# Moving 128x128 transposes of a hybrid decoder layer from TensorE to VectorE and SBUF-to-SBUF transfers

## The chip, the core and the metric

The kernel runs on one core of a Trainium2 chip. The metric is the device time of one execution in microseconds (us); the time of a kernel is the median of its runs. The core has a matrix engine (TensorE, PE in the profile), a vector engine (VectorE, DVE), a scalar engine (ScalarE, ACT), GpSimd (POOL) and SyncE (SP), which issues nearly all transfers (DMAs) here. Each engine runs its own list of instructions in order; semaphores tie the lists together.

## The reference: what is computed

One decoder layer over 2048 tokens of width 1024, in float32. After an RMS norm the tokens are projected; 4 heads of a gated linear recurrence (HGRN2, key and value width 128) and 8 heads of sliding-window attention (width 64, 2 key/value heads, window 128, one sink logit per head) run side by side; their outputs are joined, projected and added to the input. Then follow a norm, a gated MLP of width 2816 with a causal convolution of 3 tokens, and a last norm.

```python
u = rmsnorm(h, norm_mix_w[l]);  proj = u @ w_in[l]
o_hg = hgrn2_chunkwise(q_hg, k_hg, v_hg, log_f)          # S_t = diag(f_t) S_{t-1} + k_t v_t^T, o_t = S_t^T q_t
...
# attention: each block of 128 queries reads its own and the previous 128 keys; dist = query - key
scores = jnp.where((dist >= 0) & (dist < WINDOW), scores, -jnp.inf)
p = jnp.exp(scores - m);  denom = jnp.sum(p) + jnp.exp(sink - m)
out = (p / denom) @ [V_prev; V_own]
...
h = h + jnp.concatenate([o_hg, o_att], -1) @ w_out[l]
h = h + (silu(conv(v @ w_gate[l])) * (v @ w_up[l])) @ w_down[l]
```

Because the window is as long as a block, of every pair (key k of the previous block, key k of the own block) a query sees exactly one. The kernel therefore keeps one 128x128 matrix of probabilities per block and head, in which each entry belongs either to the own or to the previous block.

## The kernel before, in words

The tokens are worked in two halves of 1024 (`hf` 0 and 1). Each half has a mixing part (both kinds of heads) and then the output projection and the MLP. Large products are made of three passes over numbers split into a high and a low part (`unit`, L218: 48 matmuls of 512 columns for one 128-wide projection; `pop` in the trace is such a unit of the output projection, `g`, `q`, `f`, `hq` those of the heads).

The mixing part is cut into stages. A table `ORDER` lists them: `f`, `q`, `l`, `s`, `p` for each recurrence head (gate, query, the seven levels of the within-chunk decay, the state update, the output), `qa`, `sc`, `pv`, `pw` for each of four pairs of attention heads (query projection, scores and softmax, output of the first and of the second 512 tokens), and `g`, `v`, `w`, `m` for gates, values, weight loads and splits. The table sets priorities; a scheduler of the framework then interleaves the instructions of different stages on each engine by an estimated time line, so that the order on an engine is known only from the built program.

What the change touches:

- **Probabilities.** In `attend`, stage `sc` writes the scores into `sc` (ring `sc` of two buffers), takes the row maxima (L411), eight exponentials (L421) and normalises (L426). Stages `pv` and `pw` each turn the 128x128 matrices of one group of 512 tokens on TensorE (L435, eight transposes into `ppt`), multiply the result on VectorE by two masks (L438: `po` for the own block, `pp` for the previous one) and multiply with the values (L446, `poT`: V of the previous block with `pp`, V of the own block with `po`). `po`, `pp` and the split queries `qh`, `ql` share a ring `pp` of four buffers.
- **Keys of the recurrence.** In `hgrn`, stage `s` turns the decayed keys `K` on TensorE (L564, eight transposes into `pkn`), copies them to `Kn` on ScalarE (L565) and forms the state updates (L571, `pu`, then `SS` on VectorE, L578). Stage `p` multiplies with the values (L590 and L592, `po`), takes the norm (L593 on ScalarE, then a chain of small VectorE instructions from L173 on, then L600) and turns the result back (L605, `pot`). `ST`, `Kn` and `on` share a ring `t4` of two buffers; `SS` has one.
- **What is carried from half 0 to half 1**: the last block's keys and values, in SBUF (`kc`, `vc`).
- **Weights.** Every projection's weights come by one 512 KB load on SP's queue into `raw` (three buffers, L198), are split into `whi` and `wlo` (two buffers each) and used by 48 matmuls.

Of the kernel before, what the change touches and what calls it, by code (L numbers as in the profile page):

```python
# [8 lines left out]
F32 = mybir.dt.float32  # L9
F32R = mybir.dt.float32r  # L10
# [7 lines left out]
P = 128  # L18
# [7 lines left out]
HG = 4  # L26
# [23 lines left out]
def hymba_layer(ctx: ExitStack, tc: tile.TileContext, a: dict, out: bass.AP, rows_out: bass.AP):  # L50
# [18 lines left out]
    def ps(kind, name):  # L69
        return spaces[kind].tile([P, 512], F32, tag=kind, name=name)  # L70
# [6 lines left out]

    nmw = cp.tile([P, 16], F32, name="nmw")[:, 0:KT]
    nc.scalar.dma_start(nmw, a["norm_mix_w"])
    ones = cp.tile([P, P], F32, name="ones")  # L80
    nc.vector.memset(ones, 1.0)
# [3 lines left out]
    nc.scalar.activation(warm, ones[:, 0:1], AF.Tanh)  # L85
# [13 lines left out]
    def constants():  # L99

        C.own = cp.tile([P, P], F32, name="own")
        C.ownT = cp.tile([P, P], F32, name="ownT")
        C.prevT = cp.tile([P, P], F32, name="prevT")
        for t, op, sgn in ((C.own, ALU.is_ge, 1), (C.ownT, ALU.is_ge, -1), (C.prevT, ALU.is_gt, 1)):
# [225 lines left out]
    def across(t, base, dims):  # L330

        v = t[:, :]
        return bass.AP(v.tensor, v.offset + base, [list(v.ap[0])] + dims)

    def rows(kv):
        return slice(kv * HD, (kv + 1) * HD)

    def att_keys(hf, kv, invb, p):

        KS = p.tile([P, 2, P + HALF], F32R, name="KS")
        V = p.tile([P, 1 + TT, P], F32, name="V")
        if hf:
            nc.vector.tensor_copy(KS[:, :, 0:P], kc)
            nc.vector.tensor_copy(V[:, 0], vc)
        kT, vT = [p.tile([P, HALF], F32, tag="f", name=n, bufs=2) for n in ("kT", "vT")]
        for jj, dst in ((ATT_J, kT), (ATT_J + 1, vT)):
            o = kv[jj - ATT_J]  # L350
            for b, bs in halves():
                nc.vector.tensor_tensor(blocks(dst[:, bs], b), blocks(o[b]), blocks(invb[:, bs]), op=ALU.mult)
                nc.scalar.activation(dst[:, bs], dst[:, bs], AF.Identity, bias=C.battn[:, jj:jj + 1])
        for kv in range(2):
            r, other = rows(kv), rows(1 - kv)
            nc.scalar.copy(KS[r, kv, P:], kT[r])
            nc.vector.tensor_tensor(KS[other, kv, P:], kT[r], KS[r, kv, P:].bitcast(F32), op=ALU.subtract)
        for b in range(NB):
            pv = ps("at", "pv")
            for i in range(4):  # L360
                t0 = (b * 4 + i) * P
                nc.tensor.transpose(pv[:, i * P:(i + 1) * P], vT[:, t0:t0 + P], ident)
            nc.scalar.copy(V[:, 1 + 4 * b:5 + 4 * b].rearrange("p a b -> p (a b)"), pv)
        if hf + 1 < NH:
            nc.vector.tensor_copy(kc, KS[:, :, HALF:HALF + P])
            nc.vector.tensor_copy(vc, V[:, TT])
        return KS, V

    def attend(hf, j, X, invb, KS, V, mix, p):

        o = unit(a["w_att"][j], X, "q")
        qT = slot(f"att{j}")
# [6 lines left out]
        for g in range(NB):  # L379
# [44 lines left out]
            nc.vector.tensor_tensor(den, den, es, op=ALU.add)  # L424
            nc.vector.reciprocal(den, den)
            nc.vector.tensor_tensor(sc, sc, den.unsqueeze(3).to_broadcast([P, 2, 4, P]), op=ALU.mult)  # L426
            scs.append(sc)
        yield
        for g, sc in enumerate(scs):
            pm = []  # L430
            for kv in range(2):
                pm.append([p.tile([P, 4, P], F32, tag="pp", name=n, bufs=4) for n in ("po", "pp")])
                pt = ps("at", "ppt")
                for i in range(4):
                    nc.tensor.transpose(pt[:, i * P:(i + 1) * P], sc[:, kv, i], ident)  # L435
                ptv = pt.rearrange("p (i q) -> p i q", i=4)
                for dst, mk in zip(pm[kv], (C.ownT, C.prevT)):
                    nc.vector.tensor_tensor(dst, ptv, mk.unsqueeze(1).to_broadcast([P, 4, P]), op=ALU.mult)  # L438
            oT = ps("at", "poT")
            for i in range(4):  # L440
                n = g * 4 + i
                noprev = hf == 0 and n == 0
                for prev in (0,) if noprev else (1, 0):
                    for kv in (1, 0):
                        r = rows(kv)
                        nc.tensor.matmul(oT[r, i * P:(i + 1) * P], V[:, n + 1 - prev, r], pm[kv][prev][:, i],  # L446
                                         start=noprev or prev == 1, stop=prev == 0)
# [12 lines left out]
    def hgrn(hf, h, X, invb, vs, WG, gates, mix, p, fu=None):  # L460
# [47 lines left out]
        for m in LEVELS:  # L508
# [49 lines left out]
        Kn = p.tile([P, TT, P], F32, tag="t4", name="Kn", bufs=2)  # L558
        for b in range(NB):
            pk = ps("hg", "pkn")  # L560
            n = min(4, kept - 4 * b)
            for i in range(n):
                c = slice((b * 4 + i) * P, (b * 4 + i + 1) * P)
                nc.tensor.transpose(pk[:, i * P:(i + 1) * P], K[:, c], ident)  # L564
            nc.scalar.copy(Kn[:, 4 * b:4 * b + n].rearrange("p a b -> p (a b)"), pk[:, 0:n * P])  # L565
# [537 lines left out]
    for hf in range(NH):  # L1103
        X, kv, invb, rs, f0 = nxt
        with ExitStack() as st:
            p = pool(f"mix{hf}", stack=st, reuse_waits="tile")
            KS, V = att_keys(hf, kv, invb, p)
# [4 lines left out]
            pairs = [attend(hf, h, X, invb, KS, V, mix, p) for h in range(HG)]  # L1112
# [89 lines left out]
```

## Time and profile before

| | |
|---|---|
| time, median of 3 runs (lowest to highest) | 2150.38 us (2150.18 to 2150.38) |
| profiled execution: span from first to last instruction | 2149.0 us |
| TensorE busy | 2130.8 us (99%) |
| VectorE, ScalarE busy | 1632.2 us (76%), 1020.2 us (47%) |
| mean granted TensorE clock | 0.999 |
| transfers: all queues | 254.41 MB, mean 118 GB/s |

The profiled execution's own time is taken as its span, 2149.0 us, which is 1.4 us under the median of the runs. A group row reads: line, engine, operation, output<-inputs, shape, count | busy us in all, mean ns of one | idle time before it. A timeline or chain row reads: start us, length us, engine, what, count. Matmuls overlap in the pipeline, so the length of one matmul's row is longer than the time until the next one starts; the starts of neighbouring rows give the pace. A matmul on plain float32 data has two records in the trace for one in the program; transposes and the split products have one.

### The profile page before, as it was taken

What the parts mean: (1) busy time and instruction counts of PE and PEld (TensorE: products, weight loads), DVE (VectorE), ACT (ScalarE), POOL (GpSimd) and SP (SyncE); (2) the same over time, 40 slices, a digit from 0 to 9 for tenths busy, and PEclk for the clock granted to TensorE, in tenths of its full rate; (3) what the DMA queues carried; (4) which work ended last, traced back from release to release, by engine and by line L of the source; (5) the groups of instructions that cost most, each with busy time, mean ns of one, the idle gap of its engine ahead of it and who ended that gap; (6) DMA issues with size and microseconds to landing.
All of it is one profiled execution on the core that took longest, in us unless ns stands there. A gap on an engine that the chain in (4) does not pass through costs nothing.

```text
span 2149.0 us, 29228 instructions
## 1 busy us (share of the span) xinstructions
PE 2130.8 (99%) x11271; PEld 1790.6 (83%) x11271; DVE 1632.2 (76%) x2443; ACT 1020.2 (47%) x1818; POOL 16.2 (1%) x45
## 2 busy tenths in 40 slices
PE   8999999999999999999999999999999999999998
PEld 6988988888888888888889889888888888888887
DVE  6576768788887888785775767677988888787765
ACT  5445554564444445345634446535544444443453
POOL 2000000000000000000000000000000000000000
PEclk9999999999999999999999999999999999999999
DMA  4111012413332334974641111124223323359743
GB/s 158 40 30 40 31 30 79 137 62 125 94 122 89 103 118 147 371 255 145 217 138 40 30 31 33 40 75 158 69 104 103 118 84 122 95 187 398 236 147 133
DMA packets 91147, 254.41 MB, mean 118 GB/s; under 512 B 11136, under 2 KB 13952, under 8 KB 91008
## 3 DMA queue, kind: packets, MB, share of 16 engines
q1 hardware_dynamic: 90576, 252.29, 35.3%
q8 instruction: 88, 1.44, 0.3%
q14 instruction: 51, 0.42, 0.1%
q10 hardware_dynamic: 432, 0.27, 0.0%
HBM read 195.37 MB, written 57.15 MB: 118 GB/s over the span
## 4 chain that ended last, share of the span: by engine, by line
PE 93%; DVE 5%; ACT 1%; issue 1%; DMA 0%; SPq 0%; DVEq 0%; ACTq 0%
PE X L767 7%; PE X L766 7%; PE X L765 7%; PE pop L218 6%; PE q L218 4%; PE f L218 4%; PE hq L218 4%; PE Y L767 4%; PE Y L765 4%; PE Y L766 4%; PE pdx L954 3%; PE pdx L953 3%; PE pdx L952 3%; PE g L218 3%; PE pdy L953 3%; PE pdy L954 3%
## 5 line engine op out<-in xcount | busy, mean ns | idle before, releaser
L638 ACT CAST whi<-raw 128x1024 fp32r<-128x1024 f32 x88 | 92.7, 1053 | 115.5 <-PE X L766 71.1
L765 PE MATMUL X<-T,whi 128*128 128x512 f32 x352 | 136.9, 389 | 0.0
L766 PE MATMUL X<-T,whi 128*128 128x512 f32 x352 | 136.9, 389 | 0.0
L767 PE MATMUL X<-T,wlo 128*128 128x512 f32 x352 | 136.9, 389 | 0.0
L836 DVE SCALAR_TENSOR_TENSOR y<-ga,cw,y 128x1024 f32<-128x1024 f32 x88 | 112.7, 1280 | 25.9 <-ACT y L834 25.8
L639 DVE TENSOR_TENSOR wlo<-raw,whi 128x1024 fp32r<-128x1024 f32 x88 | 107.3, 1219 | 4.4 <-ACT whi L638 4.4
L771 ACT COPY u<-X 128x512 f32<-128x512 f32 x88 | 51.6, 586 | 122.5 <-PE X L767 122.2
L199 ACT CAST whi<-raw 128x1024 fp32r<-128x1024 f32 x58 | 60.5, 1048 | 98.8 <-issue 20.6
L639 DVE TENSOR_TENSOR xld<-raw,xhd 128x1024 fp32r<-128x1024 f32 x72 | 81.1, 1132 | 17.8 <-ACT xhd L638 17.6
L638 ACT CAST xhd<-raw 128x1024 fp32r<-128x1024 f32 x72 | 69.8, 978 | 39.1 <-DMA raw<-act0T 14.0
L218 PE MATMUL pop<-XL,whi 128*128 128x512 f32 x256 | 84.2, 392 | 0.9 <-DVE XL L230 0.9
L218 PE MATMUL pop<-XH,wlo 128*128 128x512 f32 x256 | 83.3, 391 | 0.8 <-DVE wlo L200 0.8
L218 PE MATMUL pop<-XH,whi 128*128 128x512 f32 x256 | 83.1, 396 | 0.8 <-ACT XH L229 0.5
L200 DVE TENSOR_TENSOR wlo<-raw,whi 128x1024 fp32r<-128x1024 f32 x58 | 70.5, 1220 | 9.8 <-ACT whi L199 9.8
L767 PEld LDWEIGHTS X<-T,wlo 128*128 128x128 f32 x352 | 66.1, 188 | 13.7
L766 PEld LDWEIGHTS X<-T,whi 128*128 128x128 f32 x352 | 66.1, 188 | 13.7
L765 PEld LDWEIGHTS X<-T,whi 128*128 128x128 f32 x352 | 66.0, 188 | 13.7
L630 PE MATMUL pvv<-whi,XH 128*128 128x256 f32 x256 | 73.0, 286 | 0.0
L631 PE MATMUL pvv<-whi,XL 128*128 128x256 f32 x256 | 72.9, 286 | 0.0
L632 PE MATMUL pvv<-wlo,XH 128*128 128x256 f32 x256 | 71.9, 285 | 0.0
L767 PE MATMUL X<-B,wlo 128*128 128x512 f32 x176 | 68.7, 390 | 0.7 <-DVE wlo L639 0.7
L765 PE MATMUL X<-T,Sh 128*128 128x512 f32 x176 | 68.7, 390 | 0.0
(390 smaller groups left out, 6399.2 us busy)
## 6 DMA issues: line engine op xcount, KB each, us to landing
wr<-in_w_down SPq DMA_DIRECT2D x90, 512.0 KB, 5.6
raw<-in_w_gate SPq DMA_DIRECT2D x44, 512.0 KB, 3.6
raw<-in_w_up SPq DMA_DIRECT2D x44, 512.0 KB, 3.6
raw<-act0T SPq DMA_DIRECT2D x20, 512.0 KB, 5.9
raw<-act1T SPq DMA_DIRECT2D x20, 512.0 KB, 5.6
act0B<-y SPq DMA_DIRECT2D x33, 256.0 KB, 2.3
act1B<-y SPq DMA_DIRECT2D x33, 256.0 KB, 2.4
raw<-in_w_out SPq DMA_DIRECT2D x16, 512.0 KB, 3.7
```

What stands on the lines that cost most here:

```text
L218: nc.tensor.matmul(o[b], w, x[:, bs], start=f, stop=l)
L630: nc.tensor.matmul(o[:, 0:256], xh[:, t], hi[:, c], start=kt == 0, stop=False)
L631: nc.tensor.matmul(o[:, 0:256], xl[:, t], hi[:, c], start=False, stop=False)
L632: nc.tensor.matmul(o[:, 0:256], xh[:, t], lo[:, c], start=False, stop=kt == KT - 1)
L638: nc.scalar.copy(h, src)
L639: return (eng or nc.vector).tensor_tensor(l, src, h.bitcast(F32), op=ALU.subtract)
L765: nc.tensor.matmul(o, wh[:, ws], xh, start=i == 0 and not more, stop=False, skip_group_check=more)
L766: nc.tensor.matmul(o, wh[:, ws], xl, start=False, stop=False, skip_group_check=more)
L767: nc.tensor.matmul(o, wl[:, ws], xh, start=False, stop=i == 3, skip_group_check=more)
L836: nc.vector.scalar_tensor_tensor(y, g[:, w:w + HALF], C.cw[:, ft, w:w + 1], y, op0=ALU.mult, op1=ALU.add)
L953: nc.tensor.matmul(o, wh[:, i, c], al[:, i, cols], start=False, stop=False, skip_group_check=more)
L954: nc.tensor.matmul(o, wl[:, i, c], ah[:, i, cols], start=False, stop=l, skip_group_check=more)
```

## The change

For the first three of the four pairs, the probabilities are no longer turned on TensorE. Still in stage `sc`, VectorE turns every 32x32 block in place of the whole matrix (`turned`, a block transpose from `sc` to `st`, 512 columns at a time), and 16 transfers on SP's queue (`moved`) carry the 4x4 grid of blocks of `st` to their mirrored places in `pt`. `pt` takes its buffers from the ring `sc`, `st` from the ring `pp`; no ring has grown. For the first three of the four recurrence heads the keys go the same way, at the end of stage `l`: `Kd` from the ring of `SS`, then 16 transfers into `Kn`. The last pair and the last head stay on TensorE.

The mask of the previous block is gone. With P the whole turned matrix and `po` = P masked to the own block, the output is V_prev P + (V_own - V_prev) `po`; the difference `VD` is formed once per half. The last pair, which still goes through PSUM, copies P from PSUM on ScalarE (`pw`) and masks it on VectorE.

The carried keys and values go through DRAM in place of SBUF, a constant and a mask fall away, and in `ORDER` stage `q1` now stands ahead of `pv0`.

```diff
-ORDER = ("f0 q0 l0 qa0 v0 s0 f1 p0 sc0 w0 pv0 q1 l1 qa1 pw0 g0 s1 qa2 sc1 w1 m4 f2 pv1 g1 p1 m1 q2 pw1 l2 "
+ORDER = ("f0 q0 l0 qa0 v0 s0 f1 p0 sc0 w0 q1 pv0 l1 qa1 pw0 g0 s1 qa2 sc1 w1 m4 f2 pv1 g1 p1 m1 q2 pw1 l2 "
...
-    kc = cp.tile([P, 2, P], F32R, name="kcarry")
-    vc = cp.tile([P, P], F32, name="vcarry")
+    kc = dp.tile([P, 2, P], F32, name="kcarry")
+    vc = dp.tile([P, P], F32, name="vcarry")
...
+    def moved(dst, src):
+
+        for a in range(4):
+            for c in range(4):
+                nc.sync.dma_start(dst[32 * c:32 * c + 32, :, 32 * a:32 * a + 32],
+                                  src[32 * a:32 * a + 32, :, 32 * c:32 * c + 32])
+
+    def turned(dst, src):
+
+        nc.vector.transpose(dst.rearrange("p a b -> p (a b)"), src.rearrange("p a b -> p (a b)"))
...
+        VD = p.tile([P, TT, P], F32, name="VD")
+        if hf:
+            nc.vector.tensor_tensor(VD, V[:, 1:], V[:, 0:TT], op=ALU.subtract)
+        else:
+            nc.scalar.copy(VD[:, 0], V[:, 1])
+            nc.vector.tensor_tensor(VD[:, 1:], V[:, 2:], V[:, 1:TT], op=ALU.subtract)
...
             nc.vector.tensor_tensor(sc, sc, den.unsqueeze(3).to_broadcast([P, 2, 4, P]), op=ALU.mult)
+            if j < ATT_J - 1:
+                pt = p.tile([P, 8, P], F32, tag="sc", name="pt", bufs=2)
+                for kv in range(2):
+                    t = p.tile([P, 4, P], F32, tag="pp", name="st", bufs=4)
+                    turned(t, sc[:, kv])
+                    moved(pt[:, 4 * kv:4 * kv + 4], t)
+                sc = pt
...
-                pm.append([p.tile([P, 4, P], F32, tag="pp", name=n, bufs=4) for n in ("po", "pp")])
-                pt = ps("at", "ppt")
-                for i in range(4):
-                    nc.tensor.transpose(pt[:, i * P:(i + 1) * P], sc[:, kv, i], ident)
-                ptv = pt.rearrange("p (i q) -> p i q", i=4)
-                for dst, mk in zip(pm[kv], (C.ownT, C.prevT)):
-                    nc.vector.tensor_tensor(dst, ptv, mk.unsqueeze(1).to_broadcast([P, 4, P]), op=ALU.mult)
+                own.append(p.tile([P, 4, P], F32, tag="pp", name="po", bufs=4))
+                if j < ATT_J - 1:
+                    whole.append(sc[:, 4 * kv:4 * kv + 4])
+                else:
+                    pt = ps("at", "ppt")
+                    for i in range(4):
+                        nc.tensor.transpose(pt[:, i * P:(i + 1) * P], sc[:, kv, i], ident)
+                    whole.append(p.tile([P, 4, P], F32, tag="pp", name="pw", bufs=4))
+                    nc.scalar.copy(whole[kv].rearrange("p i q -> p (i q)"), pt)
+                nc.vector.tensor_tensor(own[kv], whole[kv], C.ownT.unsqueeze(1).to_broadcast([P, 4, P]), op=ALU.mult)
...
+        Kn = p.tile([P, TT, P], F32, tag="t4", name="Kn", bufs=2)
+        if h < HG - 1:
+            Kd = p.tile([P, TT, P], F32, tag="SS", name="Kd", bufs=1)
+            turned(Kd, K.rearrange("p (c t) -> p c t", t=P))
+            moved(Kn, Kd)
         yield
...
-        for b in range(NB):
+        for b in range(NB if h == HG - 1 else 0):
             pk = ps("hg", "pkn")
```

The scheduler has made another order of all stages. Three places show it. The first is TensorE near the end of the mixing part of half 0, from the transposes of head 2's output (`pot`) on; `po` ahead of it is that head's product with values and states, `pdiag` and `plev` are the levels of the last head, `psc` the scores of the last pair. Before (its `po` rows stand 54 rows further up, with `hq`, `g` and `psc` between):

```order
L218 MATMUL g0_3224<-XH_159,wlo_3220 128x512
L605 MATMUL pot_2795<-ident_85,on_2750 128x128 x4
L218 MATMUL g1_3225<-XH_159,wlo_3220 128x512
L605 MATMUL pot_2801<-ident_85,on_2750 128x128 x4
L218 MATMUL g0_3224<-XH_167,whi_3219 128x512
L218 MATMUL g1_3225<-XH_167,whi_3219 128x512
L399 MATMUL psc_3165<-KS_447,qh_3159 128x256
```

The same place in the change:

```order
L620 MATMUL po_2922<-v_2585,ST_2251 128x128
L622 MATMUL po_2922<-SS_2900,Q_2249 128x128
L635 MATMUL pot_2964<-ident_83,on_2919 128x128 x4
L635 MATMUL pot_2970<-ident_83,on_2919 128x128 x4
L512 MATMUL pdiag_3130<-hg3_3120,K_3124 64x64 x16
L543 MATMUL plev_3149<-Q_3126,G_3150 128x2x64 x4
```

The gate units `g` of heads 2 and 3 that stood around and behind `pot` have moved ahead of it, and `pot` follows its own inputs `po` at once. From the first `pot` up to the last group of turned probabilities of the last pair (`ppt`, ahead of `pw3`), the list before has 55 matmuls of `g`, 76 of `pop` and 16 of `psc`; the list of the change has none of `g`, 30 of `pop` and 32 of `psc`.

The second place is SP's queue at pair 2 of half 0 (`raw` are weight loads, `h0` a load of the input):

```order
L196 DMA raw_3689<-in_w_out 128x1024
L337 DMA Kn_2370<-Kd_2371 32x8x32 x16
L337 DMA pt_2451<-st_2452 32x4x32 x16
L337 DMA pt_2451<-st_2470 32x4x32 x16
L337 DMA pt_2548<-st_2549 32x4x32 x16
L337 DMA pt_2548<-st_2567 32x4x32 x16
L196 DMA raw_3695<-in_w_out 128x1024
L196 DMA raw_3753<-in_w_out 128x1024
L196 DMA raw_3828<-in_w_out 128x1024
L701 DMA h0_3701<-in_xT 128x1024
```

Eighty transfers of 32 partitions stand here in one run between two weight loads; before, the weight loads followed each other.

The third is ScalarE at the second projection of values in half 0 (`v_2585` and `v_2586` receive it from PSUM; `on_2103` belongs to head 1's output, `sc_1858` to pair 1's softmax):

```order
L438 ACTIVATE es_1902<-es_1902 128x8
L623 ACTIVATE on_2103,ss_2104<-po_2106 128x128
L436 ACTIVATE sc_1858,den_1905<-sc_1858,m_1899 128x128 x8
L623 ACTIVATE on_2103,ss_2104<-po_2105 128x128
L623 ACTIVATE on_2103,ss_2104<-po_2106 128x128
L664 ACTIVATE v_2586<-pvv_2599,y_358 128x128
L664 ACTIVATE v_2586<-pvv_2626,y_358 128x128
```

The value tile `v_2586` takes the buffer of head 1's values, which head 1's last `po` frees, and its eviction now stands behind eight exponentials.

More of the change, by code (lines that the diff above doesn't have):

```diff
@@ L84, in hymba_layer @@
     warm = cp.tile([P, 32], F32, name="warm")[:, 0:1]
-    nc.scalar.activation(warm, ones[:, 0:1], AF.Tanh)
+    nc.vector.memset(warm, 1.0)
+    nc.scalar.activation(warm, warm, AF.Tanh)
     nc.gpsimd.memset(ident, 1.0)
@@ L102, in constants @@
         C.ownT = cp.tile([P, P], F32, name="ownT")
-        C.prevT = cp.tile([P, P], F32, name="prevT")
-        for t, op, sgn in ((C.own, ALU.is_ge, 1), (C.ownT, ALU.is_ge, -1), (C.prevT, ALU.is_gt, 1)):
+        for t, op, sgn in ((C.own, ALU.is_ge, 1), (C.ownT, ALU.is_ge, -1)):
             nc.gpsimd.memset(t, 1.0)
@@ L429, in attend @@
         for g, sc in enumerate(scs):
-            pm = []
+            whole, own = [], []
             for kv in range(2):
-                pm.append([p.tile([P, 4, P], F32, tag="pp", name=n, bufs=4) for n in ("po", "pp")])
-                pt = ps("at", "ppt")
-                for i in range(4):
-                    nc.tensor.transpose(pt[:, i * P:(i + 1) * P], sc[:, kv, i], ident)
-                ptv = pt.rearrange("p (i q) -> p i q", i=4)
-                for dst, mk in zip(pm[kv], (C.ownT, C.prevT)):
-                    nc.vector.tensor_tensor(dst, ptv, mk.unsqueeze(1).to_broadcast([P, 4, P]), op=ALU.mult)
+                own.append(p.tile([P, 4, P], F32, tag="pp", name="po", bufs=4))
[8 more added lines that the diff above has]
+                nc.vector.tensor_tensor(own[kv], whole[kv], C.ownT.unsqueeze(1).to_broadcast([P, 4, P]), op=ALU.mult)
             oT = ps("at", "poT")
@@ L442, in attend @@
                 noprev = hf == 0 and n == 0
-                for prev in (0,) if noprev else (1, 0):
+                for w in (1,) if noprev else (0, 1):
                     for kv in (1, 0):
                         r = rows(kv)
-                        nc.tensor.matmul(oT[r, i * P:(i + 1) * P], V[:, n + 1 - prev, r], pm[kv][prev][:, i],
-                                         start=noprev or prev == 1, stop=prev == 0)
+                        vv, pr = ((V, whole), (VD, own))[w]
+                        nc.tensor.matmul(oT[r, i * P:(i + 1) * P], vv[:, n, r], pr[kv][:, i],
+                                         start=noprev or w == 0, stop=w == 1)
             gs = slice(g * 512, (g + 1) * 512)
@@ L1111, in hymba_layer @@
             heads = [hgrn(hf, h, X, invb, vs, WG, gates, mix, p, None if h else f0) for h in range(HG)]
-            pairs = [attend(hf, h, X, invb, KS, V, mix, p) for h in range(HG)]
+            pairs = [attend(hf, h, X, invb, KS, V, VD, mix, p) for h in range(HG)]
             for name in ORDER:
```

17 lines of the change are left out of this document (7 added, 10 removed).

## The prediction

> **What bounds the kernel now.** I read the head of the page first, then TensorE's waits, then the stretch in which the change reorders most.
>
> ```profile
> span 2149.0 us, 29228 instructions
> PE 2130.8 (99%) x11271; PEld 1790.6 (83%) x11271; DVE 1632.2 (76%) x2443; ACT 1020.2 (47%) x1818; POOL 16.2 (1%) x45
> PE 93%; DVE 5%; ACT 1%; issue 1%; DMA 0%; SPq 0%; DVEq 0%; ACTq 0%
> PE kv L218 <- ACT XH L232: 6.2, 2, 5.8
> PE pop L218 <- DVE XL L230: 0.9, 2, 0.6
> ```
>
> TensorE is busy for all but 18 us of the span, the chain that ended last is 93% TensorE, and of its waits (us in all, times, longest) the largest is at the start of the keys' and values' projection, the next is 0.9 us. So a matmul that is taken away shortens the run by its own pace, as long as TensorE still has something to do in its place. And a stall of TensorE has no slack to vanish in: each us that it waits is a us of the run. The sum below is therefore a ledger of TensorE alone: work removed, against idle time added.
>
> The two stretches from `pot` of head 2 to the last `ppt` of pair 3, one in each half, read so by windows:
>
> ```profile
> core 0: us, PE busy (x) PEld busy (x) DVE busy (x) ACT busy (x) POOL busy (x), PEclk, DMA share, GB/s
> 315.23:359.53 44.30, 43.19 (x311) 35.76 (x310) 39.24 (x61) 23.41 (x60) 0.00 (x0) 1.00 0.31 96
> 1379.00:1424.81 45.81, 44.72 (x322) 37.11 (x321) 40.48 (x63) 24.56 (x63) 0.00 (x0) 1.00 0.29 92
> ```
>
> Here VectorE is busy for 39.24 of 44.30 us (0.886), ten points above its mean: the levels of head 3 and the softmax of pair 3 both run on it. TensorE idles for only 1.1 us, because `g` and `pop` stand between its dependent pieces. The two engines are nearly balanced, and this is where the change takes filler away.
>
> **Part 1, transposes removed.** 96 of the 128 `ppt` transposes and 45 of the 60 `pkn` ones go (three pairs and heads of four), 141 in all.
>
> ```profile
> L435 PE MATMUL ppt<-ident,sc 128*128 128x128 f32 x128 | 18.0, 273 | 0.0
> L564 PE MATMUL pkn<-ident,K 128*128 128x128 f32 x60 | 8.2, 273 | 0.0
> 359.46 1.09 PE L435 MATMUL ppt<-ident,sc 128*128 128x128 f32 x8
> 360.31 0.48 PE L218 MATMUL pop<-XL,whi 128*128 128x512 f32 x1
> ```
>
> A row's mean of 273 ns is a length in a pipeline. The pace is read from starts: eight transposes begin at 359.46 and the next matmul at 360.31, so one costs 0.85/8 = 0.106 us. Saving: 141 x 0.106 = 15.0 us. As an upper bound I take the busy time, 18.0/128 = 0.140 each, 19.8 us; there is no lower one beneath the pace, except the cover lost, which is counted apart.
>
> The Trainium skill, "TensorE: Matmul & The Clock Gate", Part 4, gives a 128x128 transpose some 275 ns in a kernel's context and 390 ns alone (for bf16). The trace's row length of 273 ns agrees with the first, its starts do not: they come 0.106 us apart. By 390 ns the saving would be 55 us (an estimate from that page) and the time 2135 us, that of the first rival below.
>
> **Part 2, idle at `pot`.** The new order puts `pot` of head 2 directly behind `po`. Before, 11.1 us of other matmuls lay between:
>
> ```profile
> 303.80 0.39 PE L592 MATMUL po<-SS,Q 128*128 128x128 f32 x2
> 314.90 0.60 PE L605 MATMUL pot<-ident,on 128*128 128x128 f32 x4
> L593 ACT ACTIVATE on<-po 128x128 f32<-128x128 f32 x64 | 17.7, 276 | 37.5 <-PE po L592 35.8 <-ACT whi L199 0.2
> 309.10 0.17 DVE L182 TENSOR_TENSOR t<-t,ms 128x8 f32<-128x8 f32 x1
> 309.30 0.17 DVE L183 SCALAR_TENSOR_TENSOR y<-t,y 128x8 f32<-128x8 f32 x1
> 310.10 1.29 DVE L600 TENSOR_TENSOR on<-po,y 128x512 f32<-128x512 f32 x2
> ```
>
> From `po` to `pot` there is a chain: one square on ScalarE (some 0.4 with its accumulator), twelve small VectorE instructions that start 0.20 apart (2.4), then the two products with the norm (1.29): 4.1 us. Nothing stands in TensorE's list to cover it, so 4.1 us of idle time in each half. Bounds: 4.1 if VectorE is free at once, more if other rows are ahead of it there.
>
> **Part 3, the end of the mixing part.** The order rows ahead of this text count the stretch: the list of the change has 55 matmuls of `g` and 46 of `pop` fewer, and 16 of `psc` more; it also has 16 more matmuls of `poT`, 13 of `po`, 8 of `pu`, 8 of `pkn` and 4 of `ppt`. Prices:
>
> ```profile
> 371.66 8.44 PE pop L218 x37
> 253.37 0.94 PE psc L399 x8
> 282.64 1.90 PE poT L446 x32
> 280.85 1.78 PE pu L571 x16
> ```
>
> `pop` and `g`: 8.44/37 = 0.228 each, 101 of them 23.0 us. `psc` 0.117, 16 make 1.9. A `poT` or `pu` has two records: 1.90/16 = 0.119, so 1.9; 1.78/8 = 0.223, so 1.8, and with the same price for `po` 2.9. Twelve transposes 1.3. So TensorE's work in the stretch falls from 43.2 to 43.2 - 23.0 + 9.8 = 30.0 us.
>
> VectorE's list there, from the first product behind `on` to the last mask, has 72 instructions in the change: 33 of 128x512, 5 predicated copies of 128x512, 8 of 128x256, 7 of 128x1024, 8 updates of `SS`, and 11 small ones.
>
> ```profile
> 440.23 2.41 DVE T L639 x4
> 330.83 2.24 DVE XL L230 x2
> L542 DVE COPY_PREDICATED ST<-lmask,plev 128x512 f32<-128x512 uint32 x40 | 38.3, 958 | 0.2
> L408 DVE COPY_PREDICATED sc<-own,psc 128x256 f32<-128x256 uint32 x64 | 27.6, 444 | 7.4 <-ACT sc L407 5.4 <-ACT sc L405 1.7
> L578 DVE SCALAR_TENSOR_TENSOR SS<-SS,F,pu 128x128 f32<-128x128 f32 x52 | 17.9, 344 | 1.9
> ```
>
> By pace, four of 128x512 take 2.41 (0.60 each) and two of 128x1024 take 2.24 (1.12). A mean length is some 0.09 longer than the pace, since neighbours overlap (0.17 long and 0.20 apart only for the small ones). So 33 x 0.60 = 19.8; 5 x 0.87 = 4.3; 8 x 0.36 = 2.8; 7 x 1.12 = 7.9; 8 x 0.26 = 2.0; 11 x 0.20 = 2.2: 39.0 us. If VectorE is fed as well as it was (0.886), the stretch takes 39.0/0.886 = 44.0 us. TensorE has work for 30.0 of it, against 1.1 of idle before: 44.0 - 30.0 - 1.1 = 12.9 us lost in each half. Lower bound, VectorE without any gap: 39.0 - 30.0 - 1.1 = 7.9. The filler itself isn't lost: it runs earlier, where it covers pair 2's transfers.
>
> **Part 4, idle at the values.** The second values' eviction stands behind eight exponentials on ScalarE:
>
> ```profile
> 350.75 0.41 ACT L421 ACTIVATE sc<-sc,m 128x128 f32<-128x128 f32 x1
> 353.47 0.39 ACT L421 ACTIVATE sc<-sc,m 128x128 f32<-128x128 f32 x1
> ```
>
> Seven steps take 2.72, so eight 3.1. Behind that eviction wait the PSUM buffers of `pvv` and with them TensorE. Bounds 0 (the projection comes late enough anyway) to 3.1 plus two squares, 3.5; I take 3.0, since the first `pvv` needs no eviction but all behind it do.
>
> **Part 5, edits at nothing.** *Transfers.* 480 are new, 384 of 16 KB and 96 of 32 KB, and no row before shows one of 32 partitions from SBUF to SBUF. The nearest rows:
>
> ```profile
> 2135.60 3.65 SPq L1086 DMA_DIRECT2D out<-h  x8
> out<-h SPq DMA_DIRECT2D x24, 256.0 KB, 2.4
> out<-h SPq DMA_DIRECT2D x12, 64.0 KB, 1.7
> 12.68 0.33 SPq L130 DMA_DIRECT2D sinkb<-in_sinks  x1
> 13.95 0.33 SPq L132 DMA_DIRECT2D nfw<-in_norm_ffn_w  x1
> SPq L198 <- DVE wlo L200: 470.5, 38, 37.4
> ```
>
> Eight issues of 64 KB or more take 3.65 with the last one's 0.33: a pace of 0.47, landing 1.7 us later. Below lies the issue alone, 0.33; above, the 1.27 between the starts of two small loads when the queue was crowded. I take 0.47, the row nearest in size. A group of 32 then holds SP for 15 us, and the weight loads queue behind it; but these wait 470.5 us in all for buffers, so they are mostly ahead by whole projections. *VectorE elsewhere:*
>
> ```profile
> L438 DVE TENSOR_TENSOR pp<-ppt,prevT 128x512 f32<-128x512 f32 x32 | 21.9, 684 | 0.0
> ```
>
> 32 masks go (-21.9), 24 turns of 128x512 (0.60 to 0.96, taken at a mask's 0.69) and 6 of 128x1024 (1.2) come, and two differences `VD`: +4.4 us net over the run, outside the end stretches, beside TensorE. Twelve copies `Kn` leave ScalarE (47% busy) and eight `pw` join. `kc` and `vc` through DRAM are wanted a half later. `q1` ahead of `pv0` puts 48 matmuls (48 x 0.228 = 10.9 us) before the first turned group, which covers its transfers.
>
> **Sum.** -15.0 + 2 x (4.1 + 12.9 + 3.0) = +25.0 us on the profiled 2149.0; the median of the runs stands 1.4 above it: 2150.4 + 25.0 = 2175, forecast 2176. Low end: -19.8 + 2 x (4.1 + 7.9) = +4.2, 2155. High end: pair 2's 64 transfers at 0.60 in place of 0.47, uncovered, 8.3 us in each half: 2192.
>
> **Rivals.** *The gain comes through (faster).* If in the end stretches VectorE has run ahead of its list, TensorE idles less than 7.5 us in a half and the 15.0 decide. With 0 to 3 us idle: 2135 to 2141. For it: before, TensorE found cover everywhere else. Against it: those 72 rows stand behind `on`, which needs `po`, so VectorE can't start them while TensorE is still before `pot`.
>
> *The transfers bound the pairs (much slower).* `pt` shares two buffers with `sc`, so at worst a group's softmax and turn and its 32 transfers follow one another. Softmax and turn: 3.1 of exponentials, two of 128x1024 (2.3), two turns (1.4), some six small steps (1.2), four masked scores with their copies (3): 11 us. Six groups have from the first `Kn`
>
> ```profile
> L565 ACT COPY Kn<-pkn x16: 469/586/609, 99.5 to 1427.4; 128x512 f32<-128x512 f32 x12, 128x384 f32<-128x384 f32 x4
> ```
>
> at 99.5 to `poT` of pair 2 at 282.64: 183 us. 66 + 192 p fits up to p = 0.61 us. At 0.85 it is 46 us over in each half: 2150.4 + 25 + 92 = 2267; with bounds of 0.61 and 1.27, 2190 to over 2400. For it: 1.27 above. Against it: 0.47 in the nearest row. The Trainium skill, "DMA: Bandwidth & Descriptors", Rules for kernel authors, says that under 64 KB a transfer is mostly overhead and should be joined with others, which would favour this rival; the trace agrees so far that 64 KB land in 1.7 us and 256 KB in 2.4.
>
> *A transpose is worth its length (no change).* If removing one frees 0.273 us, the saving is 38.5: 2150.4 - 38.5 + 40.0 = 2152. Against it: the starts above.
>
> **Chances.** Forecast 0.70, gain comes through 0.10, transfers bound 0.15, no change 0.05. The measurement tells 0.2% (4.3 us): faster 0.10, same 0.05, slower 0.85. The forecast's own range is 2155 to 2192; 8 times in 10 the time should lie in 2150 to 2225, which leaves out the gain and most of the transfers' case.
>
> **What would show it.** Right: 141 transposes fewer at an unchanged pace; TensorE's waits lists `pot` on `on` with about 4 us, `pvv` on ScalarE with about 3, and `plev`, `psc` or `ppt` on VectorE with 10 to 15 in each half, at the end of the mixing parts; the issues of `pt` on SP some 0.47 apart. Wrong: `poT` or `pu` waiting for DMAs in all pairs (transfers bound), raw weights late on SP (`q`, `g`, `f` waiting for loads), or TensorE busy at 99% again (gain).

## The result and the profile after

The changed kernel takes 2188.53 us (median of 4 runs, 2185.73 to 2189.51) against 2150.37: a ratio of 1.0177 (95% interval 1.0162 to 1.0191), 38.2 us slower. The forecast was 2176, its range for 8 times in 10 2150 to 2225. The sign, the place and most of the idle time were as forecast; a loss of up to 15 us to a lower clock was not in the sum.

The head of the page of the changed kernel, and its cores' clock:

```profile
span 2187.7 us, 29671 instructions
PE 2134.4 (98%) x11130; PEld 1791.8 (82%) x11130; DVE 1633.5 (75%) x2439; ACT 1017.8 (47%) x1815; POOL 19.5 (1%) x43
PE 91%; DVE 3%; ACT 2%; SPq 2%; DMA 1%; issue 0%; DVEq 0%; ACTq 0%
core 0: 2187.7 us, clock 0.992
```

The 141 matmuls are gone (11271 to 11130), but TensorE is busy for 3.6 us more than before and idle for 53.3 us in place of 18.2. More busy time for less work is the first sign of the loss that was missed; the second is the mean granted clock, 0.992 where it was 0.999.

TensorE's waits (us in all, times, longest):

```profile
PE pot L635 <- DVE on L630: 8.1, 2, 4.4
PE po L620 <- ACT on L623: 6.7, 4, 2.9
PE kv L216 <- ACT XH L230: 5.7, 1, 5.7
PE plev L557 <- DVE K L561: 3.3, 2, 2.0
PE plev L543 <- DVE Q L550: 3.2, 2, 1.7
PE pvv L660 <- ACT v L664: 3.1, 1, 3.1
PE pu L601 <- DVE sc L423: 2.9, 1, 2.9
PE pop L216 <- ACT XH L227: 2.7, 2, 2.3
PE poT L472 <- DMA pt<-st: 2.4, 1, 2.4
```

Before, only the `kv` row stood here with more than 0.9 us. `pot` and `pvv` are the two waits that the forecast named; `kv` is at the start, and most of the rest are the chains of head 3 and pair 3. Of TensorE's products only one, 2.4 us, waited for a transfer.

The end stretches (first `pot` of head 2 to the last `ppt`), one per half:

```profile
core 0: us, PE busy (x) PEld busy (x) DVE busy (x) ACT busy (x) POOL busy (x), PEclk, DMA share, GB/s
330.10:381.30 51.20, 37.72 (x315) 32.52 (x316) 40.03 (x74) 32.60 (x91) 0.00 (x0) 0.90 0.29 89
1416.50:1467.50 51.00, 39.52 (x328) 34.00 (x329) 41.29 (x78) 33.70 (x96) 0.00 (x0) 0.90 0.28 90
```

They last 51 us (44.3 and 45.8 before). VectorE is busy for 40 and 41 us, as worked out, but fills 0.78 and 0.81 of the stretch; ScalarE has 33 us where it had 23 and 25. TensorE's clock in them is 0.90.

SP's queue had a part in this too. In half 0 it issues the 16 transfers of keys and the 64 of pair 2 one after another (54 us from 286.61 on), and three weight loads stand behind them; ScalarE waits for one of these:

```profile
297.93 42.80 SPq L337 DMA_DIRECT2D pt<-st  x64
340.77 1.55 SPq L196 DMA_DIRECT2D raw<-in_w_out  x3
ACT whi L197 <- DMA raw<-in_w_out: 2.3, 1, 2.3
```

The chain that ended last runs through the end of this run of issues, some 21 us in each half (the SPq 2% of the page). How much of the 38 us that is, no run shows: run 5 has 3% on SP in its chain and is no slower than before.

**What the clock did.** Windows of 3.41 us, cut so that they fall on the times at which the clock changes:

```profile
225.13:228.54 3.41, 1.19 (x8) 0.90 (x8) 0.00 (x0) 3.41 (x21) 0.52 (x1) 1.00 0.17 27
228.54:231.95 3.41, 2.52 (x12) 2.52 (x13) 3.17 (x8) 1.60 (x9) 0.00 (x0) 0.50 0.15 24
231.95:235.37 3.42, 3.42 (x18) 3.42 (x18) 2.94 (x14) 0.42 (x2) 0.00 (x0) 0.50 0.15 24
235.37:238.78 3.41, 3.41 (x33) 3.28 (x34) 0.98 (x2) 0.83 (x3) 0.00 (x0) 1.00 0.15 24
337.77:341.18 3.41, 2.26 (x14) 1.83 (x13) 3.41 (x7) 2.72 (x6) 0.00 (x0) 1.00 0.15 24
341.18:344.59 3.41, 1.93 (x32) 1.72 (x32) 2.90 (x5) 1.19 (x2) 0.00 (x0) 1.00 0.77 225
365.08:368.49 3.41, 1.28 (x11) 1.28 (x12) 2.69 (x7) 2.08 (x10) 0.00 (x0) 1.00 0.00 0
368.49:371.90 3.41, 3.41 (x17) 3.28 (x15) 3.15 (x10) 2.11 (x10) 0.00 (x0) 0.50 0.00 0
```

The wait at `pvv` leaves TensorE idle for 2.22 of a 3.41 us window; the next two windows run at half clock (18 matmuls in 3.42 us, 33 once the clock is back). After 2.13 idle us (365.08) the next window is at half clock too; after 1.15 and 1.48 (337.77 and 341.18) it is not. All eight spells, summed:

```profile
228.54:235.37 6.83, 5.94 (x28) 5.94 (x29) 6.11 (x21) 2.01 (x11) 0.00 (x0) 0.50 0.15 24
1464.16:1467.57 3.41, 3.41 (x13) 2.94 (x12) 2.30 (x7) 0.72 (x2) 0.00 (x0) 0.50 0.22 47
sum 30.70, PE 29.55 PEld 27.54 DVE 22.84 ACT 11.51 POOL 0.52; mean PE 3.69 PEld 3.44 DVE 2.86 ACT 1.44 POOL 0.06
```

(first and last of eight, and their sum): 30.70 us at half clock, TensorE busy for 29.55 of them, so up to 14.8 us of its time was lost there. The Trainium skill, "TensorE: Matmul & The Clock Gate", Part 1, describes this gate: an idle window of about 3.4 us halves the clock. This trace agrees on the length (3.41) and the factor (0.50); the window need not be wholly idle here.

### The profile page after: what moved, and what is told of

It is laid out like the page before. It is cut to its first block, busy times and chain, and to the rows that moved or that the text cites. A ratio compares the mean times of both kernels' runs of the same rounds, so it can differ in the third digit from the quotient of the medians.

```text
span 2187.7 us, 29671 instructions
## 1 busy us (share of the span) xinstructions
PE 2134.4 (98%) x11130; PEld 1791.8 (82%) x11130; DVE 1633.5 (75%) x2439; ACT 1017.8 (47%) x1815; POOL 19.5 (1%) x43
## 2 busy tenths in 40 slices
DMA packets 173391, 264.30 MB, mean 121 GB/s; under 512 B 92608, under 2 KB 96192, under 8 KB 173248
## 4 chain that ended last, share of the span: by engine, by line
PE 91%; DVE 3%; ACT 2%; SPq 2%; DMA 1%; issue 0%; DVEq 0%; ACTq 0%
PE X L797 7%; PE X L795 7%; PE X L796 7%; PE pop L216 6%; PE q L216 4%; PE hq L216 4%; PE f L216 4%; PE g L216 4%; PE Y L796 4%; PE Y L795 4%; PE Y L797 4%; PE pdx L982 3%; PE pdx L983 3%; PE pdx L984 3%; PE pdy L982 3%; PE pdy L983 3%
```

## The experiments

Times are against the kernel before on the same chip. Theory A grows out of the prediction: the new order leaves TensorE without filler behind VectorE's chains. From run 5 on it adds a reason that the prediction didn't give: the long chain of 16 transfers from the softmax to the turned matrix, around which that order is built. Theory B puts a price on each transfer, or on the queue and the DMA engines that it holds.

**1. Probabilities only: +13.0 us** (2162.96 against 2149.95; 1.0061, 1.0045 to 1.0076). Keys stay on TensorE.

```diff
-        if h < HG - 1:
+        if h < 0:
             Kd = ...
-        for b in range(NB if h == HG - 1 else 0):
+        for b in range(NB if h >= 0 else 0):
```

> The keys of all heads stay on TensorE (their eight transposes, PSUM and ScalarE copies as before); probabilities of the first three pairs are moved as in the change. Theory A (the new order leaves TensorE without filler behind VectorE's chains, and each half loses some 19 us at the end of its mixing part): the 45 transposes of keys come back (+4.8 us), the wait at the second values falls away if its eviction stands elsewhere; in the order of this kernel the chains of head 3 and pair 3 still lack filler but pair 2 and head 2 no longer share it, so +8 to +20 us against before. Theory B (each transfer costs a fixed time on the path: 38 us plus the 15 saved over 480 transfers, 0.11 us each): 384 transfers cost 42 us, 96 transposes save 10, so +32.

A fixed price for a transfer (+32) is out; theory A's range holds the time. Its page:

```profile
span 2159.8 us, 29634 instructions
PE 2126.0 (98%) x11175; PEld 1782.5 (83%) x11175; DVE 1630.9 (76%) x2433; ACT 1022.6 (47%) x1827; POOL 19.1 (1%) x43
core 0: 2159.8 us, clock 0.999
PE psc L414 <- DVE sc L423: 4.6, 6, 1.2
```

33.8 us idle, nearly 16 more than before, but in waits of at most 1.2 us beyond the one at the start, and the clock stays at 0.999. The built list has the same 30 matmuls of `pop` and 32 of `psc` in the end stretch as the change has. So the count of filler matmuls, on which the prediction leaned, doesn't set the loss by itself: where the waits stand and how long each is matters as much. The end stretches say so by themselves (first `pot` of head 2 to the last `ppt`, as above):

```profile
321.72:366.10 44.38, 34.41 (x322) 28.73 (x321) 38.14 (x71) 31.86 (x90) 0.00 (x0) 1.00 0.27 86
1392.85:1437.30 44.45, 35.43 (x328) 29.37 (x326) 37.57 (x69) 31.78 (x92) 0.00 (x0) 1.00 0.28 86
```

Nearly the same matmuls take 44.4 us here at full clock and 51 in the change.

**2. Keys only: +15.9 us** (2165.82; 1.0074, 1.0059 to 1.0089). The mirror image, `j < 0` for the pairs.

> Only the keys of the first three heads are moved; all probabilities are turned on TensorE through PSUM (whole matrix copied by ScalarE, own block masked by VectorE). Theory A: the keys have a whole stage to land and little filler moves, so +2 to +8 us. Theory B: 96 transfers of twice the size, 10 to 20 us, less 4.8 saved: +6 to +16.

Theory A's range is missed (2 to 8); B's holds it, by its upper end. But the waits are not for transfers or loads:

```profile
PE plev L557 <- DVE K L561: 3.0, 2, 1.5
PE pkn L594 <- DVE K L561: 3.0, 2, 1.5
core 0: 2164.1 us, clock 0.997
```

The levels and the turned keys of head 3, which was not moved, wait for VectorE, and the clock falls for 10.2 us behind them. Run 3 is this kernel without the moved keys and costs 9.0, so moving them adds 6.9: by that count both ranges hold it, and the run doesn't decide between them.

**3. Values only: +9.0 us** (2158.97; 1.0042, 1.0026 to 1.0059). Nothing is moved; the new form of the values, the carry and the table stay.

> Nothing is moved by transfers: all probabilities and keys are turned on TensorE; only the new form of the values (V_prev and the difference), the copy of the whole matrix on ScalarE in place of a second mask, the carried block through DRAM, and the new place of the second query stage stay. Both theories: within 5 us of before, 0 to +4. If it is +10 or more, a part of the loss has nothing to do with the transfers.

More than twice the upper end of what both theories allowed (4). An edit that the prediction costed at nothing costs 9 us when all pairs go through PSUM. Runs 7 and 9 take it apart.

**4. One wide transfer for each 16: no difference** (2149.89; 1.0000, 0.9991 to 1.0009). The permutation of blocks is left out.

```diff
-        for a in range(4):
-            for c in range(4):
-                nc.sync.dma_start(dst[32 * c:32 * c + 32, :, 32 * a:32 * a + 32],
-                                  src[32 * a:32 * a + 32, :, 32 * c:32 * c + 32])
+        nc.sync.dma_start(dst[:, :, :], src[:, :, :])
```

> Each run of 16 transfers of 32 partitions is one transfer of 128 partitions with the same bytes, 30 in place of 480. The blocks are left where they are, so the permutation of blocks is left out of the computation; turns on VectorE, masks and matmuls are all there. The order built for it keeps gate and output projection matmuls at the end of the mixing part. Theory A: TensorE's idle time falls back to some 23 us in all, no spells at half clock, and the saving of transposes comes through: -5 to -12 us against before. Theory C (VectorE's turns and the shared buffers are what costs, not the transfers nor the order): still +10 or more.

The 38 us are gone, so turns, shared buffers and masks are not what costs (theory C is out). But nothing was gained: A's -5 to -12 is missed as well. TensorE's busy time fell by 8.1 us (2130.8 to 2122.7), not by 15.0, and idle time rose by 7.8. A expected no spell at half clock either; there is one, of 6.8 us.

**5. The same, with 450 transfers beside it: no difference** (2150.05; 1.0000, 0.9991 to 1.0010). For each wide transfer there are 15 more of 32 partitions and 16 KB that no chain waits for, from a constant in SBUF to DRAM; the permutation is left out again.

```diff
         nc.sync.dma_start(dst[:, :, :], src[:, :, :])
+        for _ in range(15):
+            names.append(0)
+            d = dp.tile([32, 4, 32], F32, name=f"side{len(names)}")
+            nc.sync.dma_start(d, ident[0:32, :].rearrange("p (h x) -> p h x", h=4))
```

> As the kernel with one wide transfer (2149.9 us, no difference to before), but behind each wide transfer come 15 transfers of 32 partitions and 16 KB, 128 bytes at a time, from a constant to a place in memory that nobody reads: 480 transfers on SP's queue as in the change, and none of the 450 extra ones is waited for by a chain. The blocks are again left where they are. Theory A (what costs is the chain from the softmax to the turned matrix, which 16 transfers at 0.6 us make 11 us long, and the order that was built around it): the time stays within 5 us of the kernel with one wide transfer. Theory B (480 transfers cost by holding SP's queue, delaying weight loads, or by crowding the DMA engines): it goes most of the way back to the change, +20 us or more against before.

Part of its timeline on SP, all 450 issues (the last two figures are the first and the last start) and their group:

```profile
120.05 10.69 SPq L341 DMA_DIRECT2D side<-ident  x21
L341 SPq DMA_DIRECT2D side<-ident x450: 302/420/1735, 19.6 to 264.4; - x150
side<-ident SPq DMA_DIRECT2D x450, 16.0 KB, 1.5
```

SP is held for 10.7 us by 21 of them, and the time doesn't move. A price for each transfer as such is out. But the run tests less than was meant. The builder put all 450 ahead of 264.4 us, in half 0, and none at the end of a mixing part, where the change's weight loads stand behind 80 issues: holding the queue costs nothing where they stand, and what it costs there stays open. Nor are they in pieces of 128 bytes, since each row of the constant is contiguous. That part is settled by the next run, as the packets of run 5, run 6 and the change show:

```profile
DMA packets 117902, 271.66 MB, mean 126 GB/s; under 512 B 18880, under 2 KB 36864, under 8 KB 117760
DMA packets 171948, 273.69 MB, mean 127 GB/s; under 512 B 87328, under 2 KB 90912, under 8 KB 171808
DMA packets 173391, 264.30 MB, mean 121 GB/s; under 512 B 92608, under 2 KB 96192, under 8 KB 173248
```

Run 6 moves nearly as many packets under 512 bytes as the change, and has almost none of its loss.

**6. Through DRAM: +2.8 us** (2152.81; 1.0013, 1.0003 to 1.0022). The complete computation, 5 transfers for 16:

```diff
+        d = dp.tile([P, n, P], F32, name=f"hop{len(names)}")
+        nc.sync.dma_start(d, src)
+        v = d.rearrange("(a r) h (c x) -> c r h a x", a=4, c=4)
+        for c in range(4):
+            nc.sync.dma_start(dst[32 * c:32 * c + 32].rearrange("r h (a x) -> r h a x", a=4), v[c])
```

> The complete computation: the turned blocks are written to DRAM by one transfer of 128 partitions and read back, with the blocks in their mirrored places, by four of 32 partitions: 5 transfers in place of 16, of them two in a row on the chain. Theory A: the chain from the turn to the matrix shrinks from 11 us to 6 (write 2, four reads 2.4, landing 2), the built order keeps most of the filler at the end, so -5 to +5 us against before. Theory B (a price for each transfer, 0.11 us): 150 transfers, +9 for the new form of the values, -15 for the transposes, +16 for the transfers: +10.

```profile
span 2149.8 us, 29267 instructions
PE 2124.7 (99%) x11130; PEld 1779.1 (83%) x11130; DVE 1635.8 (76%) x2439; ACT 1018.6 (47%) x1815; POOL 17.0 (1%) x43
hop<-st SPq DMA_DIRECT2D x24, 256.0 KB, 2.0
pt<-hop SPq DMA_DIRECT2D x96, 64.0 KB, 2.6
```

2.0 for the write and 2.6 for a read, in place of 16 issues in a row. All but 3 of the 38 us are gone with the same turns, the same values and a full permutation. This is what carries theory A: the length of the chain, with the order that the builder makes for it. The two can't be parted here, since the builder sees the shorter chain too: in half 0 its end stretch holds 75 matmuls of `pop` and 8 of `psc`, where the change has 30 and 32. Nor can they be parted from the queue, which 150 issues hold for less time than 480.

**7. Two masks as before, carry through DRAM: no difference** (2149.93; 1.0000, 0.9990 to 1.0009). As run 3, with the old masks and values.

```diff
-                nc.vector.tensor_tensor(own[kv], whole[kv], C.ownT...)
+                nc.vector.tensor_tensor(own[kv], ptv, C.ownT...)
+                nc.vector.tensor_tensor(whole[kv], ptv, C.prevT...)
...
```

> Nothing turned by VectorE, and the values as before (two masks, V of the previous and of the own block): of the change only the carried block through DRAM, the place of the second query stage and the removed constant are left. Theory A1 (the +9 us of the kernel with the new form of the values come from that form: ScalarE's copy of the whole matrix stands in the chain of the last pair, at the end of the mixing part): within 2 us of before. Theory A2 (they come from the carry through DRAM or the new place of the stage): +5 to +9 us.

The carry through DRAM and the place of `q1` are free, as costed. The 9 us are the values' new form (A1's side).

**8. Another stage table: +23.9 us** (2174.07 against 2150.22; 1.0108, 1.0093 to 1.0124). All 480 transfers as in the change; only `ORDER` differs.

```diff
-ORDER = ("f0 q0 l0 qa0 v0 s0 f1 p0 sc0 w0 q1 pv0 l1 qa1 pw0 g0 s1 qa2 sc1 w1 m4 f2 pv1 g1 p1 m1 q2 pw1 l2 "
-         "sc2 v1 m0 pv2 qa3 s2 p2 pw2 f3 m6 q3 l3 m5 sc3 g2 pv3 pw3 m2 g3 s3 p3").split()
+ORDER = ("f0 q0 l0 qa0 v0 s0 f1 w0 sc0 p0 g0 pv0 q1 l1 qa2 s1 w1 qa1 pw0 f2 sc1 g1 p1 q2 "
+         "pv1 qa3 l2 m4 pw1 sc2 pv2 f3 m1 v1 s2 m0 p2 pw2 m6 q3 m5 sc3 g2 m2 l3 pv3 g3 s3 p3 pw3").split()
```

> The change itself, all 480 transfers, turns and masks, with nothing but another stage table: scores of each pair and their outputs earlier, gate units right behind their weights, fewer stages at the end. The built order keeps 62 matmuls of the output projection between the first turned output of head 2 and the last turned probabilities of pair 3, where the change has 30. Theory A (the order in which the chains of 16 transfers are interleaved costs): a good part of the 38 us comes back, +12 to +25 us against before. Rival (the 11 us of each chain cost it in any order, or the transfers and shared buffers as such): +33 to +40.

```profile
core 0: 2172.2 us, clock 0.995
PE pot L635 <- DVE on L630: 9.3, 3, 3.7
PE plev L543 <- ACT qh L402: 5.6, 2, 2.8
```

14 of the 38 us come back by order alone, within A's range (the builder's order follows the table); the waits of 3 us and their clock spells are still there in other places.

**9. The whole matrix copied by VectorE: +2.9 us** (2153.09; 1.0014, 1.0005 to 1.0023). As run 3, but

```diff
-                    nc.scalar.copy(whole[kv].rearrange("p i q -> p (i q)"), pt)
-                nc.vector.tensor_tensor(own[kv], whole[kv], C.ownT...)
+                    nc.vector.tensor_copy(whole[kv].rearrange("p i q -> p (i q)"), pt)
+                nc.vector.tensor_tensor(own[kv], pt.rearrange("p (i q) -> p i q", i=4), C.ownT...)
```

> As the kernel with nothing moved but the values in their new form (+9.0 us), with one edit: the whole turned matrix is copied out of PSUM by VectorE in place of ScalarE, and the own block is masked from PSUM and not from that copy, so that two VectorE instructions read PSUM one after the other as in the kernel before. Theory A1 (ScalarE's copy ahead of the mask lengthens the chain from the turned matrix to its product): back to within 3 us of before. Theory A2 (the products with the difference of values, or forming that difference, cost): +6 to +9 us.

6 of the 9 us go with ScalarE's copy and its place between the turned matrix and the mask, which the edit changes at once. The 3 that are left lie between the difference of values and the copy in place of a second mask; no run parts these. In the change itself only the last pair is copied so; how much of its 38 us that costs, no run shows.

**10. Two pairs and three heads through DRAM, the old products elsewhere: -4.1 us** (2146.10 against 2150.22; 0.9981, 0.9973 to 0.9990). The complete computation; pairs 2 and 3 stay on TensorE, mask the own block from PSUM and get the previous one by subtraction.

```diff
-            if j < ATT_J - 1:
+            if j < 2:
                 pt = p.tile([P, 8, P], F32, tag="sc", name="pt", bufs=2)
...
+                    nc.vector.tensor_tensor(own[kv], ptv, C.ownT.unsqueeze(1).to_broadcast([P, 4, P]), op=ALU.mult)
+                    nc.vector.tensor_tensor(whole[kv], ptv, own[kv], op=ALU.subtract)
...
```

> The complete computation. Two pairs in place of three, and three heads, are turned by VectorE and moved through DRAM (one write of 128 partitions, four reads of 32); pairs 2 and 3 stay on TensorE with the own block masked and the previous one got by subtraction on VectorE, both from PSUM, and multiplied with the values as before. 64 + 45 = 109 transposes are saved (11.6 us). The built order keeps 53 matmuls of gates and 75 of the output projection in the end stretch. Theory A: the short chain and the filler that stays let most of the saving through: -3 to -9 us against before. Theory B (a price per transfer, or the keys' and probabilities' chains as such): 0 to +8.

```profile
span 2143.7 us, 29247 instructions
PE 2122.7 (99%) x11162; PEld 1779.9 (83%) x11162; DVE 1642.6 (77%) x2447; ACT 1013.7 (47%) x1807; POOL 18.1 (1%) x43
```

This version beats both kernels. TensorE is busy for 8.1 us less than before and idle for 2.8 more: moving the transposes does pay, by a third of the 11.6 us worked out for 109 of them, with short chains and the last two pairs on their old path.

**11 and 12. One of the two chains shortened.** Keys through DRAM, probabilities by 16 transfers: **+32.5 us** (2182.44 against 2149.91; 1.0151, 1.0136 to 1.0167). Probabilities through DRAM, keys by 16: **+16.6 us** (2166.53; 1.0077, 1.0060 to 1.0094). The edits are those of run 6, at one of its two calls (`dram` stands for run 6's function):

```diff
-                    moved(pt[:, 4 * kv:4 * kv + 4], t)
+                    dram(pt[:, 4 * kv:4 * kv + 4], t)
```

> The change with the keys alone sent through DRAM (5 transfers for each head) and the probabilities by 16 transfers of 32 partitions as in the change (384 of these). The complete computation. Theory A (the long chain of the probabilities drives the built order and the waits at the end of the mixing part): most of the loss stays, +20 to +38 us against before. Theory K (the 96 transfers of keys, twice as large, which hold the queue just ahead of pair 2's, are what hurts): it falls to +10 or less.

> The mirror image: probabilities through DRAM (5 transfers for each half group), keys by 16 transfers of 32 partitions as in the change (96 of these). The complete computation. Theory A: most of the loss goes, since a head's keys have a stage to land: +3 to +14 us against before (the kernel with both through DRAM had +2.8). Theory K: it keeps +20 or more.

```profile
core 0: 2181.7 us, clock 0.991
PE po L632 <- ACT on L635: 9.2, 6, 3.4
core 0: 2165.0 us, clock 0.996
PE po L632 <- ACT on L635: 4.6, 5, 2.6
```

(two rows of run 11, two of run 12.) Most of the loss is with the probabilities, as A has it; but with only the keys by 16 the loss is still 16.6, over A's upper end of 14, though a whole stage lies between their turn and their use. Both shortened leave 2.8. And the probabilities alone, with the keys on TensorE, cost 13.0 (run 1), with the keys through DRAM 32.5: the parts don't add. Part of that jump is the clock: 0.999 in run 1, 0.991 in run 11, where waits of 3 us return. Run 11 has the same 30 matmuls of `pop` and 32 of `psc` in its end stretch in half 0 as run 1 and the change.

## Why the prediction was right, and where it was short

- **Transposes, -15.0.** 141 are gone. Where the clock stays up, TensorE's busy time falls by less: 7.8 in run 5 (2130.8 to 2123.0), 4.8 for 96 in run 1 and 8.1 for 109 in run 10. The pace of 0.106 was read where transposes stand in a queue of ready work; where the rest of each gain went is not shown. The upper bound of 19.8, and the rival in which a transpose is worth its 273 ns, are out.
- **`pot`, 4.1 in each half.** 3.7 and 4.4: the row that sums to 8.1. Right, by the chain that was named.
- **Values, 3.0 in each half.** 3.1 in half 0. In half 1 `pvv` doesn't wait; there TensorE waits 2.9 us at `po` for ScalarE's squares: ScalarE was late there too, at another instruction, and that the size fits is luck.
- **End stretch, 12.9 in each half.** VectorE's 39.0 us of work came out at 40.0 and 41.3, and TensorE's idle time at 13.5 and 11.5 (51.20 - 37.72, 51.00 - 39.52) where 44.0 - 30.0 = 14.0 was worked out. But the stretch took 51 us and not 44, and TensorE was busy for 38 and 40 of it and not for 30: that the difference fits is two errors of some 7 us that cancel. The step that failed is "TensorE has work for 30.0 of it". Run 1 shows it at full clock: 34.4 and 35.4 us for nearly the same matmuls, so the paces priced them some 5 us too low. Run 1 also bears out the 44.0: its stretch lasts 44.4 us. In the change the clock comes on top: about 10 us of each stretch are at half clock (the clock of 0.90), up to 5 us of TensorE's time, and VectorE fell from 0.886 to 0.78. That it was fed late by TensorE and by the busier ScalarE is argued from these rows, not shown.
- **The clock, not in the sum.** Up to 14.8 us over the run. The ledger in full: -15.0 of transposes, +35.1 of idle time (53.3 - 18.2; 40.0 was forecast), up to +14.8 of half clock, and a rest of about 4: the 38.7 between the two spans. The rest hangs on the 15.0: with the 7.8 of run 5 in its place it is -3. (The sum as written, 2150.4 + 25.0, gives 2175; the forecast stood at 2176.)
- **Edits at nothing.** Carry and `q1`: right (run 7). The new values: wrong, 9.0 us where every pair uses PSUM (run 3). Queue time: not at nothing where ScalarE waits 2.3 us for a weight load behind the transfers; its full price is open. One issue took 0.60 us (median), and in the run of 64 above 42.80, 0.67 each, where 0.47 was taken:

```profile
L337 SPq DMA_DIRECT2D pt<-st x384: 585/599/1530, 122.4 to 1422.1; - x192
```

- **The rivals.** At 0.67 the pace is past the 0.61 from which the transfers were to bound the pairs, by 12 us in each half; but only one of TensorE's products waited for one, 2.4 us, so the groups do overlap, which that rival had left out. (Its lower figure, 2190, doesn't follow from its sum: at 0.61 nothing is over, and the time is 2175.) The gain did not come through.
- **The cause as told.** "Filler was pulled ahead" is half of it. Order alone is worth 14 us (run 8), but the same filler count stands in a kernel that loses 13 (run 1) and in one that loses 32.5 (run 11). The edit that takes most of the loss away is 5 transfers for 16 on each chain, with which the loss is 2.8 (run 6). Left open: how that divides between the true length of the chain, the order built for it and the time for which SP's queue is held, and why keys and probabilities together cost other than their sum.

## What to carry to other kernels

Where one engine is busy for 99%, a cheap operation taken off it pays only if its replacement isn't a longer link in a chain that the engine will wait for: cost the latency of the new path (16 issues of 0.67 and a landing of 1.8), then its throughput. Sum the idle time that a change adds per stretch, and add the clock: here each window of 3.41 us in which TensorE was idle for 2 us or more was followed by one at half clock, in which up to 1.7 us more are lost. Cost every edit that rides along, and test it alone; here one "free" edit cost 9 us where every pair took it, and the idea paid (-4.1 us) with the short chain and with two pairs on their old path. Look in the trace where the instructions of a test ended up, too: those of run 5 were not where the question was.

## What the runs showed of the hardware that was not expected

In these traces TensorE's clock changes on a fixed grid of 3.41 us: in the seven kernels with spells at half clock (the change and runs 2, 4, 6, 8, 11 and 12) all 23 spells ahead of the kernel's end start on whole steps of it and last one, two or three. Sorted by the time without a matmul, the windows of this grid at full clock in these seven show when: each of the 19 with 2.04 us or more was followed by one at half clock, four of the eleven between 1.59 and 1.93 were, and none of the more than 4,300 below. A wait of 3.11 us was thus followed by 6.83 us at half clock behind `pvv`, while run 1's idle time (33.8 us, in waits of at most 1.2 beyond the start) brought no spell (clock 0.999).

Small pieces are cheap as traffic here: run 6 moves 87,328 packets under 512 bytes, the change 92,608, and run 6 is 2.8 us slower than before. Issues that nothing waits for were free where they stood: 450 in the first 264 us, some 0.5 us apart, left the time as it was (run 5). The price of a narrow transfer from SBUF to SBUF is its issue, 0.67 us of SP's time in the change, one after another, ahead of the last one's landing and of the weight loads behind.
